# A hybrid sequence layer on one core: the next chunk's statistics move to the middle of the chunk, and products, weight maxima and the first norm are laid out anew

## The chip, the cores and the metric

The kernel runs on one core of a Trainium2 chip. The metric is the device time of one execution in microseconds. Before the change it is 1318.37 us, the median of 3 runs (1317.51 to 1323.31). The engines are named as in the profile: PE does the matrix products, DVE and POOL elementwise work, ACT activations and casts, and SP issues the DMAs. Each engine takes its own instructions strictly in the order of its queue, and waits for the others by semaphores.

## The reference, cut to what matters

One layer over x of 4096 rows by 1024 columns:

```python
h = rmsnorm(x, norm_g)
proj = h @ w_in                                 # 1024 -> 2304 columns
a_u, a_v, a_z, b_x, b_z, c_x, c_z = split(proj) # 256 each; c_x, c_z 512
ya = a_u * (masked_w @ rmsnorm(a_v) + b)        # inside blocks of 128 rows
yb = (window_mean(b_x) - b_x) @ pool_w ...      # windows of 2, 4, 8, 16 rows
yc = scan(a, gated conv4(c_x))                  # h[t] = a[t] h[t-1] + b[t]
y = concat(rmsnorm(ya)*silu(a_z), rmsnorm(yb)*silu(b_z), rmsnorm(yc)*silu(c_z))
x = x + y @ w_out
return rmsnorm(x, final_g)
```

## The kernel before, in words

The rows are taken in 8 chunks of 512. A chunk's activations lie with columns on the 128 partitions and the 512 rows along the free dimension. Each float32 factor of a large product is split into a high and a low float16 part, and a product is three float16 products (high by high, high by low, low by high). A tile of 128 output columns by 512 rows is thus 24 matmuls (8 slices of 1024, three each), made by `project` (L427). The value columns of branch a are made with rows on the partitions, by `a_values` (L588).

`mix(n, hs, prev)` is one chunk, and its order is PE's order: PE's queue is as written in the code, while a scheduler orders DVE, ACT, POOL and SP from the same code. In chunk n PE makes: the first conv tile of branch c (`c_conv`), two `a_values`, the recurrence gates of that tile (`c_gates`: two block-diagonal products, each three matmuls L434 to L436, which read `ch`, the convolved tile split by ACT L490 (high) and POOL L491 (low)), the second conv tile, the block mixing of branch a (`a_mix`, L604, which reads `th`, the normed values), the remaining tiles of u, conv and gates, then the z tiles (`gate`), the pooling branch (`b_window`, `b_mix`), and at the chunk's end the output of the *previous* chunk (`output`, L723: four blocks of 128 rows, 48 matmuls each) and, for the row norms of y, `rms_rows` (L450 and a round trip through DRAM).

What the change touches, beside that order:

- `prep_stats(n+1)` (L157 to 170) loads the next chunk's four blocks of x (L160) into the pool `big`, which has two buffers, and squares and sums each on ACT (L161). The `output` uses the same two buffers for the x it adds and for the rows it writes.
- `ybuild` (L698) splits the scaled branches (`scale_y`, L476) of a chunk into `yh` (ACT, L706) and `yl` (POOL, L707), all eight after the last output block. The output of the next chunk reads them.
- `load_group(g)` (L192) loads 256 columns of w_in, finds a bound on their size, and scales and splits them: `wh` (ACT, L236) and `wl` (DVE, L237). The bound goes through `allmax`: a product with the identity (L91), a maximum over the row on DVE (L93), a product that spreads it (L99). This happens nine times, seven of them inside chunk 0.
- `out_extent` (L368) reads w_out once for its sizes, in chunk 0; `load_out` (L376, L377) reads it again and splits it, in chunk 1. Both use `big`.
- `prep_first` squares chunk 0's eight tiles on ACT (L128) and adds them up on DVE and POOL (L133), before four small products (L138) sum over the partitions.
- PSUM has four banks for `acc` (projections and output) and four for `aux` (everything small).

Of the kernel before, what the change touches and what calls it, by code (L numbers as in the profile page):

```python
# [9 lines left out]
F16 = mybir.dt.float16  # L10
# [7 lines left out]
P = 128  # L18
# [22 lines left out]
def hybrid_kernel(ctx, tc, xT, x, w_in, w_out, par, sgu_wT, sgu_b, pool_w, gates_w, final_g, out):  # L41
# [44 lines left out]
    def allmax(dst, src):  # L86


        n = src.shape[-1]
# [9 lines left out]
        PE.matmul(ps_[:, P:P + n], ones[0:n, :], dg[0:n, 0:n], start=True, stop=True)  # L99
        V.tensor_scalar_max(dst, ps_[:, P:P + n], 1e-30)  # L100
# [19 lines left out]
    def prep_first():  # L120

        xs, sums = [], [None, None]
        for k in range(KT):
            xt = zp.tile([P, T], F32, name="hz")
            nc.sync.dma_start(out=xt, in_=xT[k * P:(k + 1) * P, 0:T])
            xs.append(xt)
            sq = work([P, T], ("a0", "a1", "t", "ti", "t", "ti", "t", "ti")[k])
# [7 lines left out]
        V.tensor_tensor(out=sums[0], in0=sums[0], in1=sums[1], op=ALU.add)  # L135
        ms = aux.tile([P, NB], F32, name="aux")
        for b in range(NB):
            PE.matmul(ms[:, b:b + 1], sums[0][:, b * P:(b + 1) * P], ones[:, 0:1], start=True, stop=True)  # L138
# [16 lines left out]

    def prep_stats(n):
        ssq = sml.tile([P, NB], F32, name="xssq")  # L157
        for b in range(NB):
            xt = big.tile([P, D], F32, name="big")
            nc.sync.dma_start(out=xt, in_=x[n * T + b * P:n * T + (b + 1) * P, :])  # L160
            A.activation(out=xt, in_=xt, func=AF.Square, accum_out=ssq[:, b:b + 1])  # L161
# [30 lines left out]
    def load_group(g):  # L192
        c0 = GROUPS[g]
# [23 lines left out]
        ma = scr("wma")  # L217
        allmax(ma, m)
        e = scr("we")
        up = 0  # L220
        if c0 in BY_SQUARES:

            V.tensor_scalar(out=e.bitcast(I32), in0=ma.bitcast(I32), scalar1=1, scalar2=0x7F800000, op0=ALU.logical_shift_right, op1=ALU.bitwise_and)
            up = 64
        else:
            exponent(e, ma)
        s = scr("ws")
        V.reciprocal(out=s, in_=e)
        V.tensor_scalar_mul(s, s, 2.0 ** (13 - up))
        V.tensor_scalar(out=ev[:, g:g + 1], in0=e, scalar1=eg, scalar2=2.0 ** (up - 22), op0=ALU.mult, op1=ALU.mult)  # L230

        V.tensor_scalar_mul(ev2[:, g:g + 1], ev[:, g:g + 1], 0.5)
        lo = wts.tile([P, KT, 256], F16, name=f"wl{g}")
        for hf in range(2):
            sl = slice(hf * 4, hf * 4 + 4)
            A.mul(out=hi[:, sl, :], in_=st[:, sl, :], mul=s)  # L236
            V.scalar_tensor_tensor(out=lo[:, sl, :], in0=st[:, sl, :], scalar=s, in1=hi[:, sl, :], op0=ALU.mult, op1=ALU.subtract)  # L237
        wgh.append(hi)
        wgl.append(lo)

# [237 lines left out]
    def gate(hs, c, y):  # L478
# [6 lines left out]
        V.tensor_tensor(out=y, in0=y, in1=th, op=ALU.mult)  # L485
# [123 lines left out]
    def a_gate(hs, y, j):  # L609
        p_ = project(hs, U0 + P * j)  # L610
        V.scalar_tensor_tensor(out=y, in0=p_, scalar=evc(U0), in1=y, op0=ALU.mult, op1=ALU.mult)
# [8 lines left out]
    def mix(n, hs, prev):  # L620
# [3 lines left out]
        def first(f, *args):  # L624
            if n == 0:
                f(*args)

        c0 = c_conv(hs, 0, n == 0)
        if n == 1:
            y_scales()  # L630
            zs, R3 = prev
            prev = ybuild(scaled(zs, *R3), False)
            for k in range(KT):
                load_out(k)
        v0 = a_values(n, hs, 0)
# [9 lines left out]
        t1 = c_gates(1, c1, p2)  # L645
        hc = c_scan(0, (t0, t1), p2)
        sqc = squares(hc, isc[:, 0:1], work([P, T], "sq"))
        first(load_group, 5)
        c2 = c_conv(hs, 2, n == 0)
        a_gate(hs, ya[1], 1)  # L650
        sqa = squares(ya, 1.0, work([P, T], "Rx"))
        first(load_group, 6)
        gate(hs, AZ0, ya[0])
        p2 = work([P, 2, T], "tr")
        t2 = c_gates(2, c2, p2)
        c3 = c_conv(hs, 3, False)
        first(load_group, 7)
# [3 lines left out]
        first(load_group, 8)  # L661
        first(pool_scale)
        if n == 0:
            with tc.issue_after(group_dma[8].ins):
                rx[1] = prep_stats(1)
        elif n + 1 < NCH:
            rx[n + 1] = prep_stats(n + 1)
        gate(hs, CZ0, hc[0])
        t3 = c_gates(3, c3, p2)
        gate(hs, CZ0 + P, hc[1])  # L670
# [4 lines left out]
        if n == 0:  # L675
            with tc.issue_after(group_dma[8].ins):
                nxt = prep_h(1, rx[1])
                for k in range(8):
                    out_extent(k)
        gate(hs, CZ0 + 2 * P, hc[2])  # L680
        yb = [b_mix(0, b0)]
        gate(hs, CZ0 + 3 * P, hc[3])
        yb.append(b_mix(1, b1))
        sqb = squares(yb, 1.0, work([P, T + 16], "a1")[:, 0:T])
        gate(hs, BZ0, yb[0])
        gate(hs, BZ0 + P, yb[1])
        if n == 0:
            return (ya + yb + hc, rms_rows((sqc, sqb), ps_)), nxt
        nxt = None
# [110 lines left out]
```

## Time and profile before

| | |
|---|---|
| three runs | 1317.51, 1318.37, 1323.31 us |
| profiled execution, its own time | 1324.18 us |
| its span | 1321.9 us |
| PE busy | 1219.5 us, 92% of the span |
| DVE, ACT, POOL busy | 740.3, 531.3, 330.7 us |
| granted TensorE clock, mean | 0.971 |

The page splits the span into 40 slices and gives the busy tenths of each engine in them:

```profile
PE   3878897999989998999979999799988999999997
DVE  6858847654555544665545554555455644755252
ACT  5665527432345224443234422543234531444121
PEclk9879997999999999999999999899999999999999
```

A slice is 33 us. The first five are chunk 0; from then on a chunk takes about four and three quarter slices, and PE dips once in each. PEclk is the clock granted to TensorE in tenths of its upper level.

### The profile page before, as it was taken

Reading aid. Unit: us, or ns where it says so; the run is one execution under the profiler, and the core shown is the slowest. Engines: PE = TensorE matmul, PEld = TensorE weight load, DVE = VectorE, ACT = ScalarE, POOL = GpSimd, SP = SyncE. Lnnn points to the kernel's source line nnn. Section 1 sums busy time; section 2 is a strip of 40 time slices with the busy share of each in tenths; the row PEclk is TensorE's granted clock in tenths of the full one; section 3 lists DMA queues with packets and bytes.
Section 4 is the critical chain, followed back from the end, with each engine's and each line's share of the span. In section 5 each row is a group of like instructions: output and inputs, shape, how many; then the busy total and the mean of one; then the engine's idle time right before and its main releaser. Section 6 shows DMA issues by size and latency. Waiting matters only on the chain.

```text
span 1321.9 us, 15392 instructions
## 1 busy us (share of the span) xinstructions
PE 1219.5 (92%) x5996; PEld 581.0 (44%) x5996; DVE 740.3 (56%) x1298; ACT 531.3 (40%) x897; POOL 330.7 (25%) x301
## 2 busy tenths in 40 slices
PE   3878897999989998999979999799988999999997
PEld 2533353444534445444444445344454444644433
DVE  6858847654555544665545554555455644755252
ACT  5665527432345224443234422543234531444121
POOL 4212224222421214212321214112242121412140
PEclk9879997999999999999999999899999999999999
DMA  9352114103210033001330023200331013100132
GB/s 329 112 139 75 56 41 150 33 3 125 99 54 8 32 112 129 8 8 57 110 113 8 0 96 105 80 8 16 113 104 48 8 32 105 64 0 1 52 103 94
DMA packets 50136, 93.74 MB, mean 71 GB/s; under 512 B 13944, under 2 KB 23544, under 8 KB 50064
## 3 DMA queue, kind: packets, MB, share of 16 engines
q1 hardware_dynamic: 50064, 92.76, 21.7%
q8 instruction: 47, 0.77, 0.2%
q14 instruction: 25, 0.20, 0.1%
HBM read 75.85 MB, written 16.89 MB: 70 GB/s over the span
## 4 chain that ended last, share of the span: by engine, by line
PE 58%; DMA 15%; DVE 11%; ACT 6%; issue 4%; POOL 4%; SPq 0%; DVEq 0%; POOLq 0%; ACTq 0%
PE acc L427 38%; PE out L723 15%; DMA big<-in_x 6%; DMA ti<-d 3%; DVE hz L476 2%; DMA d<-q 2%; DMA big<-in_w_out 2%; ACT big L161 2%; PE acc L588 1%; DVE big L735 1%; PE aux L436 1%; POOL q L465 1%; DMA out<-big 1%; PE aux L435 1%; PE aux L434 1%
## 5 line engine op out<-in xcount | busy, mean ns | idle before, releaser
L427 PE MATMUL acc<-hh,wh 128*128 128x512 f16 x896 | 344.1, 384 | 0.0
L427 PE MATMUL acc<-hl,wh 128*128 128x512 f16 x896 | 343.1, 383 | 0.0
L427 PE MATMUL acc<-hh,wl 128*128 128x512 f16 x896 | 342.3, 382 | 0.0
L427 PEld LDWEIGHTS <-wh 128*128 128x128 f16 x2048 | 201.9, 99 | 259.1 <-issue 30.5
L723 PE MATMUL out<-woh,yh 128*128 128x512 f16 x448 | 169.9, 379 | 0.0
L723 PE MATMUL out<-woh,yl 128*128 128x512 f16 x448 | 169.8, 379 | 0.0
L723 PE MATMUL out<-wol,yh 128*128 128x512 f16 x448 | 169.8, 379 | 0.0
L427 PEld LDWEIGHTS <-wl 128*128 128x128 f16 x1024 | 101.5, 99 | 128.5 <-issue 10.1
L723 PEld LDWEIGHTS <-yh 128*128 128x128 f16 x896 | 87.7, 98 | 110.7 <-issue 5.9
L484 DVE SCALAR_TENSOR_TENSOR th<-th,acc 128x512 f32<-128x512 f32 x64 | 43.7, 683 | 145.1 <-ACT th L483 145.1
L728 ACT ACTIVATE ch<-big 128x512 f16<-128x512 f32 x64 | 40.3, 630 | 209.4 <-DVE big L726 148.8
L483 ACT ACTIVATE th<-acc,ev 128x512 f32<-128x512 f32 x64 | 43.9, 686 | 127.4 <-PE acc L427 127.2
L476 DVE SCALAR_TENSOR_TENSOR hz<-hz,yc,ti 128x512 f32<-128x512 f32 x64 | 54.5, 903 | 65.1 <-DMA ti<-d 65.1
L427 PE MATMUL acc<-h,wh 128*128 128x512 f16 x256 | 82.0, 402 | 5.1 <-ACT h L151 2.6
L505 DVE SCALAR_TENSOR_TENSOR cv<-ext,cvw,cv 128x512 f32<-128x512 f32 x96 | 80.6, 839 | 2.0
L707 POOL TENSOR_TENSOR yl<-hz,yh 128x512 f16<-128x512 f32 x56 | 75.0, 1371 | 15.7 <-ACT yh L706 15.7
L183 DVE SCALAR_TENSOR_TENSOR t<-t,gp,Rx 128x512 f32<-128x512 f32 x56 | 48.1, 871 | 53.8 <-DMA t<-in_xT 41.3
L726 DVE SCALAR_TENSOR_TENSOR big<-out,so,big 128x512 f32<-128x512 f32 x64 | 47.7, 746 | 44.9 <-PE out L723 41.7
L524 POOL TENSOR_SCALAR a<-a 128x512 f32<-128x512 f32 x32 | 20.5, 640 | 207.1 <-DVE a L523 197.3
L491 POOL TENSOR_TENSOR ch<-cv,ch 128x512 f16<-128x512 f32 x32 | 37.3, 1166 | 126.4 <-ACT ch L490 90.2
L723 PEld LDWEIGHTS <-yl 128*128 128x128 f16 x448 | 43.8, 98 | 52.1
L735 DVE SCALAR_TENSOR_TENSOR big<-big,ors,fg 128x512 f32<-128x512 f32 x64 | 58.7, 957 | 13.3 <-POOL ors L732 13.3
(233 smaller groups left out, 1779.2 us busy)
## 6 DMA issues: line engine op xcount, KB each, us to landing
big<-in_x SPq DMA_DIRECT2D x60, 512.0 KB, 3.5
out<-big SPq DMA_DIRECT2D x31, 512.0 KB, 2.6
t<-in_xT SPq DMA_DIRECT2D x56, 256.0 KB, 2.8
big<-in_w_out SPq DMA_DIRECT2D x16, 512.0 KB, 3.6
st<-in_w_in SPq DMA_DIRECT2D x12, 512.0 KB, 8.3
ti<-d SPq DMA_DIRECT2D x24, 256.0 KB, 3.1
spare<-in_w_in SPq DMA_DIRECT2D x6, 512.0 KB, 5.2
hz<-in_xT SPq DMA_DIRECT2D x8, 256.0 KB, 4.9
```

Of the source, the lines that this page charges most:

```text
L183: V.scalar_tensor_tensor(out=xt, in0=xt, scalar=gp[:, k:k + 1], in1=R, op0=ALU.mult, op1=ALU.mult)
L427: PE.matmul(p_, w[g][:, k, o:o + P], h, start=(i == 0), stop=(i == 3 * KT - 1))
L476: V.scalar_tensor_tensor(out=z, in0=z, scalar=yc[:, k:k + 1], in1=R, op0=ALU.mult, op1=ALU.mult)
L483: A.activation(out=th, in_=p_, func=AF.Tanh, scale=ev2[:, g:g + 1])
L484: V.scalar_tensor_tensor(out=th, in0=th, scalar=1.0, in1=p_, op0=ALU.add, op1=ALU.mult)
L491: G.tensor_tensor(out=x2[:, 1, :], in0=v, in1=x2[:, 0, :], op=ALU.subtract)
L505: V.scalar_tensor_tensor(out=cv, in0=ext[:, k:k + T], scalar=cvw[:, 4 * j + k:4 * j + k + 1], in1=cv, op0=ALU.mult, op1=ALU.add)
L707: (V if last and False else G).tensor_tensor(out=yl[k], in0=zs[k], in1=yh[k], op=ALU.subtract)
L723: PE.matmul(po, y[k][:, b * P:(b + 1) * P], w[:, k, c * 512:(c + 1) * 512], start=(i == 0), stop=(i == 3 * KT - 1))
L726: taken.append(V.scalar_tensor_tensor(out=xc, in0=po, scalar=so, in1=xc, op0=ALU.mult, op1=ALU.add))
L728: A.activation(out=junk, in_=xc, func=AF.Square, accum_out=ssq[:, c:c + 1])
L735: V.scalar_tensor_tensor(out=xt[:, cs], in0=xt[:, cs], scalar=rs, in1=fg[:, cs], op0=ALU.mult, op1=ALU.mult)
```

## The change

It is one edit of the order and five smaller ones.

1. The statistics of chunk n+1 are cut in pieces. `stat_loads` (L168) and `stat_squares` (L177) handle two blocks after the z tile CZ0 and two after CZ0+128; a square is put behind the latest ACT instruction traced so far (`behind_last`, an ordering edge on ACT's queue, here the tanh of that gate). `out_extent` and `load_out` are tied to gates in the same way, two tiles at a time.
2. `ybuild` becomes `ypart`, called for two tiles at a time at four places early in the next chunk; the scaling is called after output block 2, and the norm rows (`rms_rows`) after block 0 instead of block 1. In the last chunk all eight parts follow the output.
3. PE's order inside a chunk: the u tile comes before the mixing, each conv tile is made before the gates of the tile before it, and the two pool products stand one z tile further apart (`hold` puts the second between a gate's product and its last multiplication).
4. `allmax` is cut in two, `maxima` (identity product and DVE maximum) and `spread`; `load_group` is cut likewise into `open_group` and the function it returns. In chunk 0 the second half of a group is called at the place of the next group (`weights`).
5. The sum of squares of chunk 0: every squared tile goes through four products with a column of ones (L139), 32 in place of 4, accumulated in PSUM; the adds on DVE and POOL are gone.

The core of the diff:

```diff
+    def maxima(src):
...
+        def spread(dst):
+            PE.matmul(ps_[:, P:P + n], ones[0:n, :], dg[0:n, 0:n], start=True, stop=True)
+            V.tensor_scalar_max(dst, ps_[:, P:P + n], 1e-30)
+        return spread
...
             A.activation(out=sq, in_=xt, func=AF.Square)
-            i = k % 2
-            if k < 2:
-                sums[i] = sq
-            else:
-                (V if i else G).tensor_tensor(out=sums[i], in0=sums[i], in1=sq, op=ALU.add)
+            for b in range(NB):
+                PE.matmul(ms[:, b:b + 1], sq[:, b * P:(b + 1) * P], ones[:, 0:1], start=(k == 0 and b == 0), stop=(k == KT - 1 and b == NB - 1))
...
+    def behind_last():
+        return tc.issue_after(next(i for i in reversed(nc.cur_bb.bb.instructions) if i.engine == mybir.EngineType.Activation))
+    def stat_loads(n, bs):
...
+                nc.sync.dma_start(out=xt, in_=x[n * T + b * P:n * T + (b + 1) * P, :])
+    def stat_squares(n, bs):
...
+            with behind_last():
+                for b in bs:
+                    A.activation(out=stats[b], in_=stats[b], func=AF.Square, accum_out=stats["s"][:, b:b + 1])
...
         c0 = c_conv(hs, 0, n == 0)
+        if n > 1:
+            y = ytiles(False)
+            parts(4, 5)
         v0 = a_values(n, hs, 0)
-        first(load_group, 2)
+        weights(2)
         v1 = a_values(n, hs, 1)
-        first(load_group, 3)
+        weights(3)
         t0 = c_gates(0, c0, p2)
+        outs(0, 1)
+        parts(6, 7)
         c1 = c_conv(hs, 1, False)
+        weights(4)
+        a_u0 = project(hs, U0)
+        parts(2, 3)
         ya = [a_mix((v0, v1), 0), a_mix((v0, v1), 1)]
-        first(load_group, 4)
-        a_gate(hs, ya[0], 0)
+        a_gate(a_u0, ya[0])
+        parts(0, 1)
+        c2 = c_conv(hs, 2, n == 0)
         t1 = c_gates(1, c1, p2)
...
+        c3 = c_conv(hs, 3, False)
         t2 = c_gates(2, c2, p2)
-        c3 = c_conv(hs, 3, False)
...
-            rx[n + 1] = prep_stats(n + 1)
         gate(hs, CZ0, hc[0])
+            stat_loads(n + 1, (0, 1))
+        stat_squares(n + 1, (0, 1))
         t3 = c_gates(3, c3, p2)
+            stat_loads(n + 1, (2, 3))
         gate(hs, CZ0 + P, hc[1])
+        stat_squares(n + 1, (2, 3))
+            rx[n + 1] = prep_stats(n + 1)
...
-            if b == 1:
+            if b == 0:
                 R3 = rms_rows((sqc, sqb), ps_)
-        return ybuild(scaled(ya + yb + hc, *R3), n == NCH - 1), nxt
+            if b == 2:
+                scaled(zs, *R3)
```

ACT's queue at the start of a chunk in the steady state, from the `yh` casts of the chunk before to the first recurrence gate. `big` is a block of x, `ext` the padded conv input, `ch` the conv tile's high half, `th` and `vssq` the value norms. Before:

```order
L706 CAST yh<-hz 128x512 x8
L728 ACTIVATE ch,ossq<-big 128x512
L161 ACTIVATE big,xssq<-big 128x1024
L500 ACTIVATE ext<-acc 128x512
L161 ACTIVATE big,xssq<-big 128x1024
L490 CAST ch<-cv 128x512
L591 ACTIVATE th,vssq<-acc,ev 128x256 x2
L161 ACTIVATE big,xssq<-big 128x1024
L591 ACTIVATE th,vssq<-acc,ev 128x256 x2
L161 ACTIVATE big,xssq<-big 128x1024
L517 ACTIVATE tr<-aux,hb,gsc 128x512
```

The same stretch of ACT's queue in the changed kernel:

```order
L794 CAST yh<-hz 128x512 x8
L815 ACTIVATE ch,ossq<-big 128x512
L537 ACTIVATE ext<-acc 128x512
L527 CAST ch<-cv 128x512
L628 ACTIVATE th,vssq<-acc,ev 128x256 x4
L554 ACTIVATE tr<-aux,hb,gsc 128x512
```

The four squares of x have left this stretch. The eight `yh` casts still stand in one row. The squares now stand in the middle of the chunk, on ACT behind three z gates (L516) and around the last recurrence gate (L554 to L557):

```order
L516 ACTIVATE th<-acc,ev_117 128x512 x3
L177 ACTIVATE big,xssq<-big 128x1024 x2
L554 ACTIVATE tr<-aux,hb,gsc 128x512
L555 ACTIVATE ti<-aux,hb,gsc 128x512
L556 ACTIVATE a_3283<-tr,spm_339 128x512
L557 ACTIVATE tr<-tr,sp_337 128x512
L516 ACTIVATE th<-acc,ev_117 128x512
L177 ACTIVATE big,xssq<-big 128x1024 x2
```

In chunk 0, ACT's queue between the first two recurrence gates. L368 reads a block of w_out, L236 writes a group's high weights, L442 squares a branch tile. Before:

```order
L161 ACTIVATE big,xssq<-big 128x1024 x2
L368 ACTIVATE big,om<-big 128x1024
L490 CAST ch<-cv 128x512
L236 ACTIVATE wh_681<-st_680,ws 128x1024 x2
L368 ACTIVATE big,om<-big 128x1024
L442 ACTIVATE Rx<-hz 128x512
L517 ACTIVATE tr<-aux,hb,gsc 128x512
L368 ACTIVATE big,om<-big 128x1024
L518 ACTIVATE ti<-aux,hb,gsc 128x512
```

The changed kernel there, from the same cast of `ch`; L235 is the first reading of a weight group:

```order
L527 CAST ch<-cv 128x512
L235 ACTIVATE wh_1023,wm_1021<-st_1022 128x512 x4
L469 ACTIVATE Rx<-hz 128x512
L537 ACTIVATE ext<-acc 128x512
L235 ACTIVATE wh_1112,wm_1111<-spare 128x512 x4
L177 ACTIVATE big,xssq<-big 128x1024 x2
L554 ACTIVATE tr<-aux,hb,gsc 128x512
L555 ACTIVATE ti<-aux,hb,gsc 128x512
```

No reading of w_out (L395 in the changed kernel) is left here; all eight stand behind z gates late in chunk 0. Two squares of x and the first readings of two weight groups stand ahead of the second gate.

PE in chunk 0, where a group's two small products stand. Before, between two projections:

```order
L427 MATMUL acc<-h_203,wl_179 128x512
L604 MATMUL aux<-swT,th 64x128 x16
L91 MATMUL aux<-ident,wm 1x128
L99 MATMUL aux<-amx,ones 128x1
L427 LDWEIGHTS wh_490
```

The changed kernel, at the end of the second conv tile and ahead of the u tile:

```order
L454 MATMUL acc<-h_224,wl_196 128x512
L105 MATMUL aux<-amx,ones 128x1
L95 MATMUL aux<-ident,wm 1x128
L454 LDWEIGHTS wh_511
L454 MATMUL acc<-h_224,wh_511 128x512
```

The pair L91, L99 of one group has become L105 of the group opened a place earlier, and then L95 of the next.

## Rows read from the trace of the kernel before

**Rows 1.** The chain of waits: start, duration (us), what; chunks 2 and 7

```profile
261.13 20.72 PE acc L427 x96
...
1043.54 20.72 PE acc L427 x96
...
1123.62 5.18 PE acc L427 x24
...
1188.98 20.72 PE acc L427 x96
```

**Rows 2.** Stretches: length, busy us (count) of PE, PEld, DVE, ACT, POOL; clock, DMA

```profile
42.70:178.20 135.50, 114.27 (x559) 54.44 (x559) 94.54 (x211) 84.18 (x145) 28.16 (x26) 0.92 0.32 92
178.20:261.10 82.90, 72.45 (x375) 36.81 (x373) 56.57 (x98) 41.50 (x64) 28.10 (x21) 0.90 0.30 89
1043.50:1189.00 145.50, 145.50 (x742) 70.46 (x740) 84.12 (x132) 55.35 (x94) 39.37 (x34) 1.00 0.14 46
```

**Rows 3.** Waits of PE from 346 to 1129 us: total, times, longest

```profile
PE aux L434 <- ACT ch L490: 24.7, 10, 3.6
PE aux L604 <- DVE th L596: 6.6, 5, 1.6
PE aux L436 <- POOL ch L491: 5.2, 10, 0.6
```

**Rows 4.** Timeline of ACT at chunk 2's start: start, us, instruction, idle time before

```profile
353.05 1.06 ACT L161 ACTIVATE big<-big 128x1024 f32<-128x1024 f32 x1 [4.79 <-DMA big<-in_x]
...
357.62 1.06 ACT L161 ACTIVATE big<-big 128x1024 f32<-128x1024 f32 x1 [2.94 <-DMA big<-in_x]
...
358.67 0.60 ACT L490 CAST ch<-cv 128x512 f16<-128x512 f32 x1
```

**Rows 5.** Timeline of all engines at the start of chunk 7

```profile
1124.35 10.94 POOL L707 TENSOR_TENSOR yl<-hz,yh 128x512 f16<-128x512 f32 x8 [2.05 <-ACT yh L706]
...
1135.93 0.62 ACT L490 CAST ch<-cv 128x512 f16<-128x512 f32 x1 [6.35 <-DVE cv L505]
...
1136.62 1.42 POOL L491 TENSOR_TENSOR ch<-cv,ch 128x512 f16<-128x512 f32 x1 [0.38 <-ACT ch L490]
...
1139.12 0.38 PE L434 MATMUL aux<-ch,gh 128*128 128x512 f16 x1
```

**Rows 6.** Waits of PE from 178 to 261 us

```profile
PE aux L604 <- DVE th L596: 5.9, 3, 4.7
PE aux L434 <- ACT ch L490: 3.6, 1, 3.6
```

**Rows 7.** Waits of PE from 42 to 178 us

```profile
PE aux L99 <- DVE amx L93: 8.3, 7, 5.0
PE aux L434 <- ACT ch L490: 8.0, 3, 4.5
PE aux L436 <- POOL ch L491: 3.0, 4, 1.6
```

**Rows 8.** Timeline of ACT in chunk 0, at a reading of w_out

```profile
83.22 1.06 ACT L368 ACTIVATE big<-big 128x1024 f32<-128x1024 f32 x1 [4.42 <-DMA big<-in_w_out]
```

**Rows 9.** Timeline of DVE in chunk 0

```profile
90.67 2.48 DVE L237 SCALAR_TENSOR_TENSOR wl<-st,ws,wh 128x1024 f16<-128x1024 f32 x2 [1.05 <-ACT wh L236]
93.06 0.27 DVE L93 TENSOR_REDUCE amx<-aux 1x1 f32<-1x128 f32 x1
```

**Rows 10.** Timelines of ACT and of PE in the first 18 us

```profile
4.14 1.27 ACT L128 ACTIVATE a<-hz 128x512 f32<-128x512 f32 x2 [2.15 <-DMA hz<-in_xT]
...
10.59 0.63 ACT L128 ACTIVATE ti<-hz 128x512 f32<-128x512 f32 x1 [0.43 <-DMA hz<-in_xT]
...
16.18 1.87 PE L138 MATMUL aux<-ones,a 128*128 128x1 f32 x8
```

**Rows 11.** The chain of waits at the end: start, duration (us), what

```profile
1226.54 11.91 PE out L723 x56
...
1276.75 37.98 PE out L723 x170
```

More of the change, by code (lines that the diff above doesn't have):

```diff
@@ L126, in prep_first @@
             xs.append(xt)
-            sq = work([P, T], ("a0", "a1", "t", "ti", "t", "ti", "t", "ti")[k])
+            sq = work([P, T], ("a0", "a1", "t", "t", "ti", "ti", "a0", "a1")[k])
             A.activation(out=sq, in_=xt, func=AF.Square)
-            i = k % 2
-            if k < 2:
-                sums[i] = sq
-            else:
-                (V if i else G).tensor_tensor(out=sums[i], in0=sums[i], in1=sq, op=ALU.add)
+            for b in range(NB):
+                PE.matmul(ms[:, b:b + 1], sq[:, b * P:(b + 1) * P], ones[:, 0:1], start=(k == 0 and b == 0), stop=(k == KT - 1 and b == NB - 1))
         load_group(0)
[L135 to L138, printed above, removed]
         rs = sml.tile([P, NB], F32, name="xrs")
@@ L620, in mix, with weights, parts @@
     def mix(n, hs, prev):
-        def first(f, *args):
+        opened = []
+        def weights(g, f=None):
             if n == 0:
-                f(*args)
+                if opened:
+                    opened.pop()()
+                if f:
+                    f()
+                if g is not None:
+                    opened.append(open_group(g))
+        zs, y = prev if prev else (None, None)
+        def parts(*ks):
+            if n:
+                for k in ks:
+                    ypart(zs, y, k)
@@ L660, in mix @@
         rms_row(ps_, 2, sqa)
[L661 to L666, printed above, removed]
+        gate(hs, CZ0, hc[0])
+        weights(8)
+        nxt = None
+        late = tc.issue_after(group_dma[8].ins) if n == 0 else ExitStack()
+        with late:
+            stat_loads(n + 1, (0, 1))
+        stat_squares(n + 1, (0, 1))
+        t3 = c_gates(3, c3, p2)
+        late = tc.issue_after(group_dma[8].ins) if n == 0 else ExitStack()
+        with late:
+            stat_loads(n + 1, (2, 3))
+        gate(hs, CZ0 + P, hc[1])
+        stat_squares(n + 1, (2, 3))
+        if n + 1 < NCH:
             rx[n + 1] = prep_stats(n + 1)
-        gate(hs, CZ0, hc[0])
-        t3 = c_gates(3, c3, p2)
-        gate(hs, CZ0 + P, hc[1])
+        weights(None, pool_scale)
         hc += c_scan(1, (t2, t3), p2)
@@ L677, in mix @@
                 nxt = prep_h(1, rx[1])
-                for k in range(8):
-                    out_extent(k)
         gate(hs, CZ0 + 2 * P, hc[2])
+        extents(0, 1)
+        gate(hs, CZ0 + 3 * P, hc[3])
+        extents(2, 3)
         yb = [b_mix(0, b0)]
-        gate(hs, CZ0 + 3 * P, hc[3])
-        yb.append(b_mix(1, b1))
+        gate(hs, BZ0, yb[0], hold=lambda: yb.append(b_mix(1, b1)))
         sqb = squares(yb, 1.0, work([P, T + 16], "a1")[:, 0:T])
-        gate(hs, BZ0, yb[0])
+        gated(yb[0])
@@ L695, in mix @@
                 R3 = rms_rows((sqc, sqb), ps_)
-        return ybuild(scaled(ya + yb + hc, *R3), n == NCH - 1), nxt
-    def ybuild(zs, last):
-        if last:
-            yh, yl = ([t[:, k, :] for k in range(KT)] for t in hkeep)
-        else:
-            th = yp.tile([P, KT, T], F16, name="yh", tag="yh")
-            tl = yp.tile([P, KT, T], F16, name="yl", tag="yl")
-            yh, yl = ([t[:, k, :] for k in range(KT)] for t in (th, tl))
-        for k in (4, 5, 6, 7, 2, 3, 0, 1):
-            A.copy(out=yh[k], in_=zs[k])
-            (V if last and False else G).tensor_tensor(out=yl[k], in0=zs[k], in1=yh[k], op=ALU.subtract)
-        return yh, yl
+            if b == 2:
+                scaled(zs, *R3)
@@ new lines, in mix, with ytiles, ypart @@
+        if n == NCH - 1:
+            y = ytiles(True)
+            for k in YORDER:
+                ypart(zs, y, k)
+        return (zs, y), nxt
+    YORDER = (4, 5, 6, 7, 2, 3, 0, 1)
+    def ytiles(last):
+        if last:
+            return [[t[:, k, :] for k in range(KT)] for t in hkeep]
+        ts = [yp.tile([P, KT, T], F16, name=nm, tag=nm) for nm in ("yh", "yl")]
+        return [[t[:, k, :] for k in range(KT)] for t in ts]
+    def ypart(zs, y, k):
+        A.copy(out=y[0][k], in_=zs[k])
+        G.tensor_tensor(out=y[1][k], in0=zs[k], in1=y[0][k], op=ALU.subtract)
```

119 lines of the change are left out of this document (74 added, 45 removed).

## The prediction

> **What bounds the kernel now.** I read the page's first part, its slices, then the waits of PE, then stretches of one chunk, then timelines. PE works 1219.5 of 1321.9 us, in an order that is fixed, so time is won only where PE stands idle, or runs at a low clock. The slices show one dip of PE in each chunk and a ragged first five slices.
>
> The chain gives the length of a chunk. Its row with 96 products of L427 starts chunk 2's late part at 261.13 and chunk 7's at 1043.54: five chunks, 782.41 us, 156.48 each. The same row returns at 1188.98 at the end of chunk 7: 145.44 us [rows 1]. What is different in chunk 7 is that no chunk follows, so no statistics are prepared in it. In that stretch PE is busy all of 145.50 us at a clock of 1.00 [rows 2]: this is the kernel with the dip gone, with PE's work for a chunk unchanged.
>
> The dip's cause is in the waits. Between 346 and 1129 us PE waits 24.7 us for ACT's `ch` (L490), 6.6 for `th`, 5.2 for POOL's `ch` (L491): 36.5 us [rows 3]. Chunk 2's timeline shows why. ACT stands 4.79 and 2.94 us before two of the squares L161, each waiting for a block of x, and the cast of `ch`, 0.60 us, runs as soon as the last of these is done [rows 4]. A block can be loaded only when the output of the chunk before releases one of the two `big` buffers. So x's loads delay the cast, and the cast delays the first gate's products. The difference 156.48 − 145.44 = 11.04 a chunk is more than the 7.3 of waiting; the rest is low clock and refill after the gaps.
>
> **The change part by part.**
>
> *Statistics to mid-chunk.* The same 28 squares of 1.06 us stay on ACT, but leave the place where PE waits for ACT. Their new place is behind tanhs of the last z gates, where the output buffers have been free for many microseconds: the next use of them is the output at the chunk's end, one position later. For five chunks, 2 to 6, the gain is 5 × 11.04 = 55.2 us, if the chunk becomes the one of chunk 7. What is late next? In chunk 7 `ch` high is done at 1135.93 + 0.62 = 1136.55 and low at 1136.62 + 1.42 = 1138.04, and the product that reads high starts at 1139.12 [rows 5]: about 1 to 2.6 us in hand. Before it stand POOL's eight `yl`, 10.94 us. The order shows that these eight and their `yh` still stand in one row in later chunks, so parts two at a time do not shorten this; they also do not lengthen it. The conv tile made before the gates, and norm rows one output block earlier (some 10 us), add cover. I price the step at −55, between −28 (half the waits stay) and −60.
>
> *Chunk 1.* The stretch 178.2 to 261.1 takes 82.9 [rows 2]; the same work in chunk 7 goes from 1123.62 to 1188.98, 65.4 [rows 1]. 17.5 us are lost, of which 5.9 and 3.6 are waits for `th` and `ch` [rows 6] and the rest low clock (0.90) and refill. The two readings of w_out and the squares leave this place. A small part remains: w_out's own maximum products, and a wait or two for them, together some 3 us. Price −14, between −6 and −16.
>
> *Chunk 0.* 42.7 to 178.2 is 135.5 us [rows 2]. A whole undisturbed chunk less an output (8 × 5.18) and one conv tile (5.18) would be 145.44 − 41.4 − 5.2 = 98.8, with 5.18 for 24 products [rows 1]. So 36.7 are lost: the three waits of 8.3, 8.0 and 3.0 [rows 7], a clock of 0.92 (8% of 135.5 is 10.8), refill. Two causes go. The readings of w_out leave ACT: one of these stands 4.42 us for its DMA [rows 8], and the cast of `ch`, the gate's tanh and the wh of the next group stand behind them. And the group's second product (L99, now L105) no longer follows L91 at once, but stands a projection later; this alone is worth up to 8.3. What is late next: DVE is in order, and the maximum of a group stands behind two splits of the group before, 2.48 us that wait for ACT's wh [rows 9]. Walking the new order by these durations I get, as an estimate, 3.6 us of wait at the first L105 behind the next group's weights, 2.9 at the one after, and some 6 us in front of the second pool product late in chunk 0, because the eight w_out readings now stand there and their loads queue on SP behind the squares' tiles. So about 12.5 of the waits come back. Price −12, between −22 (they don't) and +5 (a w_out wait that shows twice, at the pool product and at chunk 1's weights).
>
> *First sum of squares.* It adds 28 small products, each two passes. Four products are 8 passes in 1.87 us, 0.234 each; 64 passes are 15.0 us. The first square starts at 4.14 and takes 0.635, so PE would end no earlier than 19.8, against 16.18 + 1.87 = 18.05 before: +1.7. But the adds leave DVE and POOL, and the last square ends at 11.22 [rows 10]; if the passes keep up with the squares, PE ends within a microsecond or so, −5. As PE is idle otherwise and the weights' own path is about as long, I take 0, range −5 to +2.
>
> The Trainium skill ("TensorE: Matmul & The Clock Gate", section LDWEIGHTS (loading the stationary operand)) says a load takes about its columns over 1.2 ns, 107 ns for 128. By that 64 passes would be 6.8 us, hidden under the squares, and the sum would be 5 us lower; no row here shows 107 ns for a float32 pass, and the row of 0.234 decides for me. What it would give is inside the rival "faster start" below.
>
> *Tail.* From 1226.54 to the last product's end, 1276.75 + 37.98 = 1314.73, are 88.2 us [rows 11]. Eight output blocks are 384 products at 5.18/24 = 0.216: 82.9. Norm products take about 1.3; 4.0 are lost. The norm rows start one block earlier and the y of the last chunk is there sooner: −4, between −4 and 0.
>
> *Wider spacing of the other products* (u before the mixing, conv before gates): the same products, and chunk 7 shows them without waits already, so 0 by itself, and cover for the parts above.
>
> **Sum.** −55 − 14 − 12 − 4 + 0 = −85. On the profiled execution, 1324.18, that is 1239. This execution was 5.8 above the median of the three runs, so on the median it is 1233. The terms come from the profile and the comparison is against the runs; I put the forecast between, at 1236.
>
> **The rivals.**
>
> *Start-up gains nothing* (12 lost of the sum): the second halves of the groups stand behind DVE's splits, and the w_out loads merely move the wait to the end of chunk 0. For it: the 2.48 us of splits ahead of the maximum [rows 9], the SP queue. Against: 8.3 us of wait directly behind L91 that spacing must shorten [rows 7]. Gives 1236 + 12 = 1248.
>
> *Half of the chunk start's waits stay.* Chunk 7 has 1 to 2.6 us in hand, and in it neither loads nor stores of a following chunk compete; its DMA share of 0.14 [rows 2] already holds the output, though. If in chunks 2 to 6 `ch` comes 2 us later than in chunk 7, a gap with its low clock reopens in each. Half of 55 is 27.6: 1264. This also is the case that the y parts don't do what they say, since the eight casts in one row then are what is late.
>
> *Faster start.* The first sum ends 5 us earlier and the waits in chunk 0 don't come back (−22 in place of −12): 1236 − 15 = 1221 to 1224.
>
> *Slower.* The squares are tied behind the tanh of the z gates CZ0 and CZ0+128. If the x tile is not there when ACT reaches the square, ACT stands, and the tanhs of later z gates behind it, which empty PE's `acc` banks. There are four banks at 5.18 us a tile, so PE has some 15 us before it stops. To be slower than before, more than 85 us must return, over seven chunks 12 us each past those 15: a load that is 27 us late. For it: in the same queue of SP these loads stand among others, and such waits were 4.79 us at most in chunk 2 [rows 4]. Against: both `big` buffers are free here, and the second pair's loads need only the first pair's two squares to be done. It would give 1325 or more.
>
> **How the numbers follow.** The forecast gets 0.61 (own range 1226 to 1246), start-up gains nothing 0.16, half stays 0.10, faster start 0.09, slower 0.04. The range 1221 to 1262 leaves out most of the half case, a little of the faster start and the slower one: 0.17. About 0.5%, 6.6 us, is what a measurement of this kernel can tell from no change. Faster takes all but the slower case and a thin part between: 0.94; within 0.5% 0.03; slower 0.03.
>
> **What would show it.** In the changed profile the chain's row of 96 products should come every 145 to 147 us from chunk 2 on, and no wait of PE for ACT's `ch` should be left there. If it comes every 150, the y casts and POOL are late next. Between the two, wait rows of PE for `th` mark the mixing. In chunk 0 the waits at L105 for DVE should be 3 to 7 us in sum and one for the pool product near 150; chunk 1's first conv tile should start near 166, not 178. The tail from the last z tile should be 84 to 85 us. If ACT shows idle time at the squares (L177) with PE waiting for a bank, the slower case has come; if the first norm ends before 14 us, the faster start has.

## The result and the profile after

The changed kernel takes 1277.74 us (median of 4 runs, 1273.16 to 1278.22) against 1320.28 for the kernel before: a ratio of 0.967, interval 0.9636 to 0.9703. That is 43 us less, half of the 85 forecast, and above the range of 1221 to 1262. Its profiled execution, 1273.16 us, is the fastest of the four; its span of 1271.3 is 50.6 below the span before.

The chunks tell where the gain is. A stretch here goes from the first value product (L588 before, L625 now) of one chunk to that of the next; the last one goes to the end. Before, in us: 42.7 ahead of chunk 0, then 141.8 (chunk 0 to 1), 161.8 (1 to 2), 782.4 (five stretches, to chunk 7), 193.3. The same stretches of the changed kernel, with the columns of [rows 2]:

```profile
43.16:179.59 136.43, 119.47 (x581) 56.50 (x581) 96.41 (x212) 84.96 (x145) 32.34 (x26) 0.91 0.27 88
179.59:336.46 156.87, 150.18 (x745) 72.39 (x744) 104.01 (x167) 66.71 (x109) 48.84 (x35) 0.98 0.28 86
336.46:1080.31 743.85, 732.31 (x3702) 352.51 (x3701) 430.80 (x670) 293.25 (x506) 197.65 (x175) 1.00 0.20 64
1080.31:1271.30 190.99, 182.19 (x909) 86.78 (x907) 94.67 (x148) 60.67 (x110) 48.13 (x43) 1.00 0.15 52
```

The differences are: start +0.5, chunk 0 −5.3, chunk 1 −4.9, the five later ones −38.6, the end −2.3. A second profile of the same kernel (the control below, span 1279.6) has −5.1, −1.8, −33.5 and −2.2 for the last four, so the single numbers are good to a few us. A later chunk takes 148.8 us in place of 156.5; the undisturbed one of [rows 1] is 145.4. So 3.3 us a chunk are still lost, and most of chunk 0's and chunk 1's losses are. What PE waits for, from 336 to 1080 us and then from 43 to 180:

```profile
PE aux L463 <- POOL ch L528: 8.2, 13, 0.8
PE aux L461 <- ACT ch L527: 3.0, 4, 1.3
...
PE aux L461 <- ACT ch L527: 10.0, 3, 7.5
PE aux L463 <- POOL ch L528: 5.7, 3, 4.4
PE acc L625 <- DVE wl L265: 0.8, 1, 0.8
```

The waits on `ch` that [rows 3] had are down from 29.9 to 11.2 us. The 11.2 us left are in two places: 5.7 at the first recurrence gate of a chunk, and 5.5 at the two pool products, where the kernel before had none. In chunk 0 the waits for `amx` of [rows 7], 8.3 us, are gone, but those for `ch` have grown from 11.0 to 15.7.

The chain of waits names the cause of the first remainder. These are its pieces at the end of chunk 6 (start, us, what):

```profile
1049.30 1.80 DMA d<-tr
...
1051.12 1.76 DMA q<-d
...
1053.16 2.29 POOL q L492
...
1055.46 3.71 DMA d<-q
...
1059.24 3.43 DMA ti<-d
...
1064.10 2.00 DVE hz L503 x3
...
1070.55 1.34 DVE big L822 x2
...
1071.90 2.64 DMA out<-big
...
1074.56 3.50 DMA big<-in_x
...
1079.64 4.24 ACT yh L794 x8
...
1084.51 0.49 ACT ext L537
```

Read downwards: the norm rows go through DRAM and come back; DVE scales the branches (L503); only then it norms and stores an output block (L822); only then a `big` buffer is free for the x of the last block; the sum with that x holds ACT up; and behind it stand the eight `yh` casts and the `ext` of the next chunk's conv tile. DVE's own timeline at the end of chunk 1:

```profile
310.77 0.75 DVE L813 SCALAR_TENSOR_TENSOR big<-out,so,big 128x512 f32<-128x512 f32 x1 [0.55 <-PE out L810]
319.49 4.07 DVE L503 SCALAR_TENSOR_TENSOR hz<-hz,yc,ti 128x512 f32<-128x512 f32 x6 [7.97 <-DMA ti<-d]
323.47 0.21 DVE L817 TENSOR_SCALAR ors<-ossq 128x1 f32<-128x1 f32 x1
...
334.39 1.41 DVE L813 SCALAR_TENSOR_TENSOR big<-out,so,big 128x512 f32<-128x512 f32 x2 [2.07 <-DMA big<-in_x]
```

DVE stands 7.97 us for the rows while the norm of block 1 (L817), whose sums of squares ACT had done at 312.3, is queued behind. The second remainder, at the pool products, is of the same kind. In chunk 2, on DVE:

```profile
421.49 1.42 DVE L202 SCALAR_TENSOR_TENSOR t<-t,gp,Rx 128x512 f32<-128x512 f32 x2 [5.18 <-DMA Rx<-rxd]
422.82 0.75 DVE L602 SCALAR_TENSOR_TENSOR ext<-a,prm,ext 128x512 f32<-128x512 f32 x1
```

And on SP's queue, the store and the reading of the row of the statistics:

```profile
405.85 1.36 SPq L802 DMA_DIRECT2D big<-in_x  x2
408.19 0.38 SPq L185 DMA_DIRECT2D rxd<-xrs  x1
417.02 0.33 SPq L187 DMA_DIRECT2D Rx<-rxd  x1
```

The first two products of the next chunk's h (L202) stand ahead of the pool window (L602) and wait 5.18 us for the row of the statistics. The statistics are now made so late that their round trip through DRAM, 13 us from L185 to the first use, reaches into this place. The kernel before has the same wait, but shorter (12.5 us in all its chunks together, 35.1 now), and in chunk 2 it stands 17 us ahead of the first window.

### The profile page after: what moved, and what is told of

The parts are those of the page before. It is cut to its first block, busy times and chain, and to the rows that moved or that the text cites. A ratio compares the mean times of both kernels' runs of the same rounds, so it can differ in the third digit from the quotient of the medians.

```text
span 1271.3 us, 15561 instructions
## 1 busy us (share of the span) xinstructions
PE 1213.9 (95%) x6052; PEld 589.5 (46%) x6052; DVE 752.5 (59%) x1294; ACT 524.9 (41%) x897; POOL 338.9 (27%) x298
## 5 line engine op out<-in xcount | busy, mean ns | idle before, releaser
L454 PE MATMUL acc<-hh,wh 128*128 128x512 f16 x896 | 340.5, 380 | 0.0
L202 DVE SCALAR_TENSOR_TENSOR t<-t,gp,Rx 128x512 f32<-128x512 f32 x56 | 47.0, 849 | 75.2 <-DMA t<-in_xT 40.1
L561 POOL TENSOR_SCALAR a<-a 128x512 f32<-128x512 f32 x32 | 26.7, 833 | 240.3 <-DVE a L560 237.9
L542 DVE SCALAR_TENSOR_TENSOR cv<-ext,cvw,cv 128x512 f32<-128x512 f32 x96 | 86.2, 898 | 2.5
L795 POOL TENSOR_TENSOR yl<-hz,yh 128x512 f16<-128x512 f32 x56 | 72.2, 1328 | 41.1 <-ACT yh L794 41.1
L503 DVE SCALAR_TENSOR_TENSOR hz<-hz,yc,ti 128x512 f32<-128x512 f32 x64 | 47.7, 803 | 58.2 <-DMA ti<-d 58.2
L516 ACT ACTIVATE th<-acc,ev 128x512 f32<-128x512 f32 x64 | 43.7, 682 | 74.1 <-PE acc L454 69.8
L819 POOL TENSOR_TENSOR ors<-ors,mhalf 128x1 f32<-128x1 f32 x32 | 21.0, 656 | 176.7 <-DVE ors L818 176.7
L528 POOL TENSOR_TENSOR ch<-cv,ch 128x512 f16<-128x512 f32 x32 | 44.8, 1399 | 71.6 <-ACT ch L527 65.8
```

The costliest lines, as they stand in the source:

```text
L202: V.scalar_tensor_tensor(out=xt, in0=xt, scalar=gp[:, k:k + 1], in1=R, op0=ALU.mult, op1=ALU.mult)
L454: PE.matmul(p_, w[g][:, k, o:o + P], h, start=(i == 0), stop=(i == 3 * KT - 1))
L503: V.scalar_tensor_tensor(out=z, in0=z, scalar=yc[:, k:k + 1], in1=R, op0=ALU.mult, op1=ALU.mult)
L516: A.activation(out=th, in_=p_, func=AF.Tanh, scale=ev2[:, g:g + 1])
L528: G.tensor_tensor(out=x2[:, 1, :], in0=v, in1=x2[:, 0, :], op=ALU.subtract)
L542: V.scalar_tensor_tensor(out=cv, in0=ext[:, k:k + T], scalar=cvw[:, 4 * j + k:4 * j + k + 1], in1=cv, op0=ALU.mult, op1=ALU.add)
```

## The experiments

Theory A: what is left are in-order stands of DVE behind a round trip through DRAM. Rivals: B, the eight casts in a row are late by themselves; C, the pool products wait because of their new place; D, the spacing and the y parts carry the gain and the statistics do not. The first eight runs stand beside kernels before of 1325 to 1327 us, where the changed kernel again took 1281.23 (0.966), the last four beside 1317.

**Scalings behind output block 2.**

```diff
-            output(n - 1, y, (b,))
+            taken = output(n - 1, y, (b,))
...
             if b == 2:
-                scaled(zs, *R3)
+                with tc.issue_after(taken[-1].ins):
+                    scaled(zs, *R3)
```

> The changed kernel, with the eight scalings of the branches (L503) tied behind the sums of output block 2 on DVE; the same work in another order on DVE. Theory A (DVE stands in its queue for the norm rows' round trip through DRAM, ahead of block 1's norm, so the x of block 3 is loaded late and everything behind it on ACT): the waits of PE for ch at the start of a chunk (1.0 to 1.4 us for the high half and 0.65 for the low) go, a chunk becomes 2 to 2.5 us shorter, and the time falls by 12 to 17 us against the changed kernel, to 1261 to 1266. Rival B (the eight casts yh and eight differences yl in one row are late by themselves, whatever DVE does): within 2 us of the changed kernel, 1276 to 1280, with the waits in place.

1265.38 us, ratio 0.9564 (0.9538 to 0.959): 16 less than the changed kernel's 1281.23, 13 by the ratios. Later chunks take 147.7. At the end of chunk 1 DVE now norms block 1 ahead of the scalings, and does not stand for them:

```profile
316.73 0.21 DVE L818 TENSOR_SCALAR ors<-ossq 128x1 f32<-128x1 f32 x1 [0.85 <-ACT ch L816]
...
326.16 4.05 DVE L503 SCALAR_TENSOR_TENSOR hz<-hz,yc,ti 128x512 f32<-128x512 f32 x6
```

In the five later chunks PE has no wait at the first gate any more, and 8.9 us at the pool products. Rival B falls: the casts are in one row as before.

**h behind the pool windows.**

Here `wins[1]` is the second pool window (the second L602 of a chunk).

```diff
-        V.scalar_tensor_tensor(out=pf, ...)
+        wins[j] = V.scalar_tensor_tensor(out=pf, ...)
...
-                nxt = prep_h(n + 1, rx[n + 1], range(4 * b, 4 * b + 4), nxt)
+                with tc.issue_after(wins[1].ins):
+                    nxt = prep_h(n + 1, rx[n + 1], range(4 * b, 4 * b + 4), nxt)
```

> The changed kernel, with the products that make the next chunk's h (L202) tied behind the second pool window on DVE, where two of them stood ahead of the first window and waited 5.2 us for the row of the statistics. Theory A (DVE in order behind a round trip): the waits at the pool products (0.2 and 0.8 us a chunk, up to 2 in chunk 1) go, a chunk becomes 1 to 1.5 us shorter, in all 6 to 10 us less than the changed kernel, 1268 to 1272. Rival C (the pool products wait because of their new place in PE's order): no change, 1276 to 1280.

1260.78, ratio 0.9529 (0.9508 to 0.9551): 20 less, 17 by the ratios, about twice what I expected. Later chunks are 146.8 (148.8 in the changed kernel, 149.8 in its control run), chunk 1 155.6. Rival C falls: no wait at the pool products is left in the later chunks, though they stand where they stood. Why the gain is more than these waits can be read in part from the five later chunks of the control and of this kernel:

```profile
339.69:1088.57 748.88, 732.41 (x3701) 352.47 (x3700) 430.69 (x670) 292.74 (x505) 196.91 (x176) 1.00 0.19 63
```

```profile
334.38:1068.55 734.17, 728.53 (x3702) 352.14 (x3701) 425.96 (x670) 294.30 (x507) 198.22 (x176) 1.00 0.20 65
```

Of the 14.7 us between them 6.7 are the waits at the pool products, 4.0 are waits at the first gate (9.6 became 5.6), and 3.9 are shorter busy time of PE for the same products. Why the gate's waits fall with the tie was not traced.

**The move of the statistics alone, on the kernel before.**

```diff
...
-        elif n + 1 < NCH:
+        gate(hs, CZ0, hc[0])
...
+            stat_loads(n + 1, (0, 1))
+        stat_squares(n + 1, (0, 1))
+        t3 = c_gates(3, c3, p2)
...
+            stat_loads(n + 1, (2, 3))
+        gate(hs, CZ0 + P, hc[1])
+        stat_squares(n + 1, (2, 3))
+        if n + 1 < NCH:
             rx[n + 1] = prep_stats(n + 1)
-        gate(hs, CZ0, hc[0])
-        t3 = c_gates(3, c3, p2)
-        gate(hs, CZ0 + P, hc[1])
```

> The kernel before with the move of the statistics alone (two blocks behind the z gate CZ0, two behind CZ0+P). Theory: it is this move that shortens the later chunks, 156.5 to about 149, and nothing else of the change is needed: 35 to 45 us less than the kernel before, 1275 to 1285. Rival D (the move alone only shifts the waits, and the y parts and the wider spacing of PE's products are what removes them): under 20 us of gain, over 1300.

1320.16, ratio 0.9963 (0.9948 to 0.9978): nearly nothing, a clear miss of my theory, and what rival D had forecast. The waits at the chunk's start are gone, but one at the first pool product has come. Waits of PE from 356 to 1123 us:

```profile
PE aux L451 <- ACT ch L507: 24.2, 5, 5.8
```

DVE ahead of such a wait, the first h products and the window behind them:

```profile
438.82 1.42 DVE L200 SCALAR_TENSOR_TENSOR t<-t,gp,Rx 128x512 f32<-128x512 f32 x2 [4.79 <-DMA Rx<-rxd]
440.15 0.74 DVE L582 SCALAR_TENSOR_TENSOR ext<-a,prm,ext 128x512 f32<-128x512 f32 x1
```

The later chunks take 153.4 us, 3.1 less than before, and chunks 0 and 1 are 3.7 and 6.7 longer. The move alone thus carries the wait from the first gate (29.9 us before, none now) to the pool product (none before, 25.0 now, both for five chunks).

**The change without the move.**

```diff
         weights(8)
...
-            stat_loads(n + 1, (0, 1))
-        stat_squares(n + 1, (0, 1))
...
+        elif n + 1 < NCH:
+            rx[n + 1] = prep_stats(n + 1)
         t3 = c_gates(3, c3, p2)
...
-            stat_loads(n + 1, (2, 3))
         gate(hs, CZ0 + P, hc[1])
-        stat_squares(n + 1, (2, 3))
```

> The changed kernel with the statistics made in one piece at the old place in the code, all else as changed. If the statistics carry the gain of the later chunks: chunks of about 155 to 157 us, 1310 to 1318. Rival D (spacing and y parts carry it): under 1295.

1289.07, ratio 0.9737 (0.9716 to 0.9758). So all else brings 36 us without the move, as rival D has it; but only 15 of these come in the five later chunks, and 19 in chunk 0, where the other edits of the change lie. Later chunks are 153.4, with 26.3 us of waits at the first gate and none at the pool products; chunk 1 is 162.0. Chunk 0 is shorter than with the move by 14 us, and at nearly full clock:

```profile
43.14:165.46 122.32, 112.52 (x581) 54.71 (x581) 96.34 (x212) 85.55 (x145) 30.97 (x26) 0.99 0.32 98
```

**The move and the tie of h, on the kernel before.** The kernel of the third experiment with the edit of the second:

```diff
-                nxt = prep_h(n + 1, rx[n + 1], range(4 * b, 4 * b + 4), nxt)
+                with tc.issue_after(wins[1].ins):
+                    nxt = prep_h(n + 1, rx[n + 1], range(4 * b, 4 * b + 4), nxt)
```

> The kernel before with the move of the statistics, and with the first products of h (L202's like) tied behind the second pool window on DVE. The move alone left one wait of 4.3 to 5.8 us a chunk, at the first pool product. Theory A (that wait is DVE's, which stands in its queue for the row of the statistics ahead of the windows): it goes, chunks 2 to 6 fall from 153.2 to 145.5 to 147.5 us, the time by 35 to 45 us against the move alone, to 1275 to 1285. Rival (the first pool product follows its window too closely in PE's order, and only the wider spacing helps): chunks stay at 152 or more, over 1305.

1273.15, ratio 0.96 (0.9572 to 0.9628), a little below what I gave, and 8 less than the whole change. From 351 to 1079 us PE has no wait left; columns as above:

```profile
351.38:1078.94 727.56, 727.55 (x3701) 352.24 (x3700) 435.09 (x671) 296.44 (x505) 202.87 (x176) 1.00 0.21 65
```

727.56 over five is 145.5, the undisturbed chunk, without y parts and without new spacing. Rival D falls for these chunks: the rest of the change had only covered part of DVE's stand.

**Control.** The changed kernel, with no edit.

> The changed kernel itself, once more, as the measure for the runs beside it on the same chip: 0.967 of the kernel before, about 1281 us where that takes 1325.

1281.23, ratio 0.966 (0.9629 to 0.9691), as expected.

**Both ties.** The diffs of the first and the second experiment together.

> The changed kernel with both ties (scalings behind output block 2, h behind the pool windows). If the two waits are apart from each other: the gains add, 14 and 20 us, 1243 to 1252 where the kernel before takes 1325, and chunks 2 to 6 are 145.4 to 146.2 us, as the undisturbed chunk. If they are one wait counted twice: as the better of the two, about 1260.

1254.61, ratio 0.9457 (0.9428 to 0.9486). Chunks 2 to 6:

```profile
334.73:1061.98 727.25, 727.25 (x3702) 352.28 (x3700) 426.89 (x671) 295.76 (x505) 197.75 (x176) 1.00 0.21 65
```

Every one is 145.45. The median is 2.6 above the end of what I gave; the two gains overlap by 3 to 9 us.

In the five later chunks (us) the kernels so far compare like this; PE's busy time and its waits make up the stretch:

| kernel | stretch | PE busy | waits at the first gate | waits at the pool products |
|---|---|---|---|---|
| before | 782.4 | 745.9 | 29.9 | 0 (6.6 at the mixing) |
| before, with the move | 767.0 | 742.0 | 0 | 25.0 |
| before, with the move and the tie of h | 727.6 | 727.6 | 0 | 0 |
| changed, without the move | 767.1 | 740.9 | 26.3 | 0 |
| changed (control) | 748.9 | 732.4 | 9.6 | 6.7 |
| changed, scalings tied | 738.6 | 729.6 | 0 | 8.9 |
| changed, h tied | 734.2 | 728.5 | 5.6 | 0 |
| changed, both ties | 727.3 | 727.3 | 0 | 0 |

**Chunk 0 as before, too.** The kernel with both ties; in chunk 0 the four squares are made in one piece and lose the tie to ACT's gate.

```diff
...
+        if n == 0:
+            with tc.issue_after(group_dma[8].ins):
+                for b in range(NB):
+                    stat_loads(1, (b,))
+                    stat_squares(1, (b,), False)
+                rx[1] = prep_stats(1)
+        else:
             stat_loads(n + 1, (0, 1))
-        stat_squares(n + 1, (0, 1))
+            stat_squares(n + 1, (0, 1))
...
```

> As the kernel with both ties, and chunk 0 prepares the statistics of chunk 1 in one piece as before the change, tied only behind the last weight group's load. Without the move the first chunk took 122.3 us in place of 136.4. Theory E (in chunk 0 the move costs time, since the second pair of squares is late and h, casts and pool windows stand behind it): 10 to 14 us less than the kernel with both ties, chunk 0 at 122 to 127. Rival (the first chunk gained from the whole of chunk 1's work staying at its old place, not from its own): chunk 0 at 133 or more, within 4 us of the kernel with both ties.

1238.70, ratio 0.9335 (0.9307 to 0.9364), the lowest ratio of all: 42 us less than the changed kernel, and 16 less than with both ties, a little more than I gave. The rival falls, since chunk 0 itself is shorter:

```profile
43.32:165.75 122.43, 114.97 (x581) 55.48 (x581) 96.19 (x212) 85.12 (x145) 30.97 (x26) 0.96 0.31 99
165.75:319.82 154.07, 149.26 (x745) 71.31 (x744) 103.30 (x168) 71.49 (x117) 53.69 (x39) 0.98 0.30 90
```

With the move DVE stood in chunk 0, too. Here is the first L202 of the kernel with both ties, and below it the first two of this kernel, without idle time:

```profile
143.14 0.75 DVE L202 SCALAR_TENSOR_TENSOR t<-t,gp,Rx 128x512 f32<-128x512 f32 x1 [4.13 <-DMA Rx<-rxd]
```

```profile
110.73 1.41 DVE L202 SCALAR_TENSOR_TENSOR t<-t,gp,Rx 128x512 f32<-128x512 f32 x2
```

The last four start from this kernel (below: the base; span 1236.6) and change one part each. Their kernel before was 0.7% faster, but their later chunks are the same 145.45 us, so a ratio of the other runs doesn't carry over; I compare spans and stretches, and a median only where it agrees.

**First sum of squares as before.**

```diff
-            for b in range(NB):
...
-                PE.matmul(ms[:, b:b + 1], sq[:, b * P:(b + 1) * P], ones[:, 0:1], ...)
...
+                (V if i else G).tensor_tensor(out=sums[i], in0=sums[i], in1=sq, op=ALU.add)
```

> The kernel with both ties and chunk 0's old statistics (0.9335 of the kernel before, 1238.7 us where that takes 1326.8), with the first sum of squares as before the change (adds on DVE and POOL, four products). The prediction priced this edit at 0, between -5 and +2. Its traces show the first value product at 43.2 us with the products of squares and at 42.7 with the adds: theory, no difference, within 2 us of 0.9335 of the kernel before, and the first value product within 1 us of 43.3. Rival (POOL and DVE freed early matter further on in chunk 0): 3 us or more slower than with the products.

1239.15 us, ratio 0.9403 (0.9377 to 0.9428); span 1235.7. The ratio is above the 0.9335 that I gave, which by itself would speak for the rival; the stretches don't: the first value product comes at 41.35 in place of 43.32 (earlier than I gave), chunk 0 takes 123.1 (122.4), chunk 1 154.0 (154.1), the end 190.0 (189.5). In sum 0.9 less: no use and no harm that can be told.

**Groups whole again.**

```diff
-                    opened.append(open_group(g))
+                    open_group(g)()
```

> The same base, with the second half of each weight group called at once, so that its two small products stand beside each other in PE's order again. Theory F (what chunk 0 gained besides the statistics is the halves: the wait of 8.3 us between the two products, with its low clock): 8 to 16 us slower than the base, 0.940 to 0.946 of the kernel before, chunk 0 at 131 to 138 us, waits of PE for amx back. Rival (the w_out readings were the cause): under 4 us.

1245.05 us, ratio 0.9446 (0.9422 to 0.947); span 1243.2, +6.6, less than the 8 to 16 that I gave, but the rival falls. Chunk 0 takes 127.8, +5.4. The waits are back, though for `amx` smaller than the 8.3 us of [rows 7]:

```profile
PE aux L105 <- DVE amx L97: 6.0, 5, 2.0
PE aux L105 <- DVE wm L239: 4.0, 4, 2.9
```

**w_out's sizes early again.**

```diff
-                    for k in ks:
-                        out_extent(k)
+                    pass
...
                 nxt = prep_h(1, rx[1])
+                for k in range(8):
+                    out_extent(k)
```

> The same base, with all eight sizes of w_out read at the old place in the code, free to stand where the scheduler puts them early in chunk 0. Theory G (they delay the cast of ch and the gates' tanhs on ACT as in the kernel before, waits of 2.4 and 4.4 us): 4 to 12 us slower in chunk 0, and 1 to 2 us back in chunk 1 as the sizes are there sooner; 0.936 to 0.942. Rival (with the groups in halves ACT has room for them): within 3 us of the base.

1246.23 us, ratio 0.9457 (0.943 to 0.9483); span 1244.0, +7.4: chunk 0 +10.4 (132.9), as theory G has it, chunk 1 −2.6. PE's largest wait in chunk 0:

```profile
PE aux L461 <- ACT ch L527: 12.5, 2, 9.9
```

ACT at a reading of w_out, as in [rows 8]:

```profile
88.78 1.06 ACT L395 ACTIVATE big<-big 128x1024 f32<-128x1024 f32 x1 [4.95 <-DMA big<-in_w_out]
```

**Norm rows of chunk 0 behind the first conv tile of chunk 1.**

Here `c0[2]` is the last DVE operation (L542) of that tile.

```diff
...
             y_scales()
-            scaled(zs[0], *zs[1])
+            with tc.issue_after(c0[2]):
+                R3 = rms_rows(*zs[1])
+            scaled(zs[0], *R3)
...
-            return ((zs, rms_rows((sqc, sqb), ps_)), None), nxt
+            return ((zs, ((sqc, sqb), ps_)), None), nxt
```

> The same base, with the norm rows of chunk 0 made behind the first conv tile of chunk 1, on PE and on DVE. In the changed kernel DVE stands 6.2 us for their round trip, ahead of that conv tile. Theory A: the waits of PE for the sizes of w_out and for ch at the start of chunk 1 (1.5 and 3.0 us) go, with their low clock: 4 to 8 us less than the base, 0.927 to 0.931 of the kernel before. Rival (the conv tile is late for ACT's or POOL's sake): within 2 us of the base.

1245.12 us, ratio 0.9453 (0.9427 to 0.9479); span 1245.5, +8.9: a miss of the wrong sign. The wait of 1.5 us for w_out's sizes went (0.6 is left), but the round trip now ends later, and the six scalings stand ahead of the second conv tile:

```profile
188.49 6.77 DVE L503 SCALAR_TENSOR_TENSOR hz<-hz,yc,ti 128x512 f32<-128x512 f32 x6 [3.69 <-DMA ti<-d]
195.18 4.27 DVE L404 SCALAR_TENSOR_TENSOR wol<-big,os,woh 128x1024 f16<-128x1024 f32 x2
...
203.89 1.37 DVE L540 TENSOR_SCALAR cv<-ext,cvw,cvb 128x512 f32<-128x512 f32 x1
```

PE then waits 10.5 us for `ch`. It is theory A's mechanism again, produced by an edit that was to remove it.

## Why the prediction was wrong

*What was right.* The undisturbed chunk is real: chunks of 145.45 us, five in a row, as soon as two edges hold DVE's order. (The rows at 261.13 and 1043.54 that the prediction puts in chunks 2 and 7 lie late in chunks 1 and 6, since chunk 2 starts at 346.23; the five starts of a chunk between them are those of chunks 2 to 6, so its sum stands.) The old cause, squares waiting for x on ACT at the chunk's start, went with the move. The sum of −85 was what the parts could give: the base of the last four runs takes 1238.7 beside 1326.8, which is −88, with the two ties and chunk 0's statistics at their old place. That the sum is so near is in part luck: by stretches the later chunks give the −55 exactly, but chunk 0 gives −19 for −12 and chunk 1 −8 for −14. Spacing and y parts, priced at 0 by themselves, are worth nothing in the later chunks once DVE's order is held (145.5 without them, 145.45 with them). Without the ties they do count: all that the change has besides the move takes 3.1 us off a later chunk without the move, and about 4 with it.

*Statistics to mid-chunk, −55: measured −38.6.* The step failed at "What is late next?". I looked for it only where the old wait had been, at the chunk's start, and in a stretch that ends in chunk 7, which prepares no statistics and so cannot show what late statistics hold up. I did not follow the moved chain to its reader: the row Rx passes through SP and DRAM, and L202 needs it on DVE, ahead of the pool windows. The norm rows one output block earlier, which I counted as cover, came with `scaled` a block earlier, too, and so the scalings stood on DVE ahead of block 1's norm, and the x of the last block came late; with the scalings tied behind block 2 the early norm rows do no harm. My rival "half of the chunk start's waits stay" had the place of one of the two waits, and the eight y casts with POOL's `yl` as its cause; holding scalings back, with the casts as they were, removed it.

*Chunk 0, −12: measured −5.3.* The two causes named are real. Of the base's chunk 0, the place of w_out's readings carries 10.4 us and the halves 5.4. What I left out is the move itself: with its pairs of squares tied to ACT's queue chunk 0 took 13.6 more (136.05 with both ties, 122.43 with the squares of chunk 0 in one piece and free; these two were not changed apart). The waits of 3.6 and 2.9 that I walked at the first L105s did not come: 0.7 is all that PE waits there. The wait that I did foresee, in front of the second pool product, came (7.5 us), and I gave its cause to the readings of w_out. One of these does stand in its way, with ACT idle for 2.38 us before it at 158.91; but without the move, and with those readings in the same order, 1.5 is left of it.

*Chunk 1, −14: measured −4.9, and −1.8 in the control.* In the base it is −7.7. The prediction lets the two readings of w_out leave this place. Only the second one stood there (L376, 187.5 to 219.6 us), and it is still there in the changed kernel (L403, 203.3 to 246.6); the first one has moved to the end of chunk 0, and PE now waits 2.4 us for its maximum at the start of chunk 1. How much of the rest can be had is open: the norm rows' round trip was in the way in both places where it was tried.

*First sum, 0: measured 0.* The products cost 2.0 us in the start (I had 1.7), of which chunk 0 and the end give back 1.1; the 0.9 left is less than the runs can tell. Here are sixteen passes in the changed kernel with their weight loads, and the eight passes of the old sum:

```profile
8.40 3.55 PE L139 MATMUL aux<-ones,t 128*128 128x1 f32 x16
```

```profile
4.96 3.49 PEld L139 LDWEIGHTS aux<-ones,a 128*128 128x128 f32 x16 [0.66 <-ACT a L136]
```

```profile
15.90 1.87 PE L145 MATMUL aux<-ones,a 128*128 128x1 f32 x8
```

A pass takes 0.222 us, near the 0.234 of [rows 10], and a load 0.218. The 107 ns that the Trainium skill gives for a load of 128 columns ("TensorE: Matmul & The Clock Gate", section LDWEIGHTS (loading the stationary operand)) are not seen in these rows.

*Tail, −4: measured −4.3.* From the last z tile to the end of the span (to the last product, where the prediction stopped, 88.2 became 84.0):

```profile
1226.54:1321.90 95.36, 85.86 (x388) 37.45 (x386) 38.19 (x59) 17.44 (x42) 19.47 (x17) 0.97 0.24 86
```

```profile
1180.22:1271.30 91.08, 83.97 (x389) 37.46 (x386) 38.12 (x59) 17.39 (x42) 19.47 (x17) 0.99 0.26 90
```

The stretch of −2.3 above begins at chunk 7's first value product; chunk 7's own part became 2.0 longer, with 1.6 us of waits for `ch` that the kernel before did not have there.

*The range.* Its upper end took in part of a case in which half of the waits stay; that the moved chain makes new waits in every chunk was in no rival. The slower rival put the danger on ACT, at the squares; DVE was where it lay.

## What to carry to other kernels

When a chain is moved later, follow it to its last reader, and ask what stands behind that reader on its engine: a consumer of a round trip belongs behind everything that does not need it. A stretch that lacks the moved work shows what can be won, but not what the work will hold up in its new place. A scheduler can put such a consumer first. One ordering edge was worth more than the waits that it was put against: in five chunks 14.7 us against 6.7.

## What was not expected of the hardware

POOL's subtraction for the low half took 4.91 us in chunk 0 of the changed kernel, where 32 of them mean 1.40; DVE ran two scans of 1.26 us each beside it. The wait of PE behind it was 4.4 us. In the base, where the order on these engines is another, the same subtraction starts at 90.76 and takes 1.20. What slowed it was not tested.

```profile
91.75 4.91 POOL L528 TENSOR_TENSOR ch<-cv,ch 128x512 f16<-128x512 f32 x1 [1.27 <-ACT ch L527]
```
